# Layer 1's input projection with tokens on partitions: its two products turned in 32x32 blocks through DRAM, and the last projection begun two column blocks wide

## The chip, the cores and the metric

The kernel runs on one core of one Trainium2 chip. A time is the device time of one launch in microseconds (us). The verdict compares medians of runs of the two kernels taken on the same chip. Three runs of the kernel before gave 1809.98, 1813.17 and 1820.33 us.

The engines are named as in the profile: PE is the matrix engine (PEld its weight loads), DVE the vector engine, ACT the scalar engine, POOL and SP the other two. SP and ACT each have a hardware DMA queue; 16 DMA engines serve both. A name like L416 is line 416 of the kernel whose profile is quoted.

## What is computed

One step of a two-layer diffusion backbone over 256 latent tokens of width 2048. Layer 0 (neighbourhood attention and a state-space scan side by side) is not touched. Layer 1 is a gated short convolution:

```python
def short_conv_mixer(h, w_in, conv_w, w_out):
    p = h @ w_in                                  # (256, 2048) by (2048, 8192)
    bg, cg, hv, g = jnp.split(p, 4, axis=-1)
    y = bg * dw_conv(cg * hv, conv_w)             # 3 taps along the tokens
    return (jax.nn.silu(g) * y) @ w_out           # (256, 2048) by (2048, 2048)
...
x = x + gate[:, None] * y
```

All inputs and the output are fp32.

## The kernel before

**Products.** Every fp32 operand is split into a high part, rounded to the matrix engine's reduced fp32 format, and a low part, the difference. A product is three matmuls: high by high, low by high and high by low. Weights stream from DRAM in chunks of 512 KB (two blocks of 128 input rows by 512 columns) into one of five `raw` buffers; ACT makes the high part (`wH`, L409) and DVE the low part (`wL`, L416); three pairs of `wH`/`wL` buffers alternate. A chunk's low part frees the `raw` buffer, and the next load, issued on SP, goes into it. A chunk's last matmul frees its `wH` and `wL`, for the cast three chunks later.

**Two ways to multiply.** `mm_act` holds a block of 128 tokens of the activations as the stationary operand and streams 512 weight columns: tokens come out on the partitions, and a chunk takes 2 x 2 x 3 = 12 matmuls of 512 columns. `mm_both` holds a 128 x 128 weight block and streams the activations, high and low side by side (512 columns), and then the low weights against the high activations (256 columns): channels come out on the partitions, and a chunk takes 2 x 4 x 2 = 16 matmuls, half of 512 columns and half of 256. Layer 1's input projection uses `mm_both`; its results need channels on the partitions, since the convolution runs along the tokens. The output projection uses `mm_act`.

**Layer 1 before.** For each of four blocks `i` of 512 channels and each of the four parts (cg, hv, bg, g) the loop at L1770 takes four banks and eight chunks. `both` (L1715) empties a bank: ACT copies one half, DVE adds the other. `hv_gen` forms u = hv cg and the convolution into `v`, `bg_gen` multiplies by bg, `gg_gen` by silu(g) and splits the result into `y2` (high by ACT, L1766; low by DVE, L1767). The output projection (L1796) takes four column blocks of 512 one after the other, eight chunks each; its inner index is the channel block, so it needs the last channels' `y2` from its seventh chunk on.

**What sets the order.** The program is written in one pass. `Plan` keeps an estimated clock for each engine and for the data; generators hand out their steps when the clocks say that these are due (`may`, `pump`), and `force` drives them when a chunk can't go on. On the chip each engine then keeps the order that was written. Two details matter below. `Plan.keys` follows DRAM tiles in units of 256 elements, so two writes that share such a unit are planned one after the other. And beside layer 1's weights a matrix-vector product runs in the background (`gemv_gen`, L788): its blocks, 512 KB of `in_ada_w` each, share the `raw` buffers, and DVE multiplies them into `acc` (L803 before, L806 after, two instructions a block).

Of the kernel before, what the change touches and what calls it, by code (L numbers as in the profile page):

```python
# [10 lines left out]
AF = mybir.ActivationFunctionType  # L11
ALU = mybir.AluOpType
# [3 lines left out]
KB = 16  # L16
# [21 lines left out]
class Plan:  # L38
# [32 lines left out]
    def cost(self, e, op, i, ins, outs):  # L71
        n = max(self.size(a) for a in ins + outs)
        if e == "PE":
            n, cols = self.size(outs[0]), outs[0].ap[0][1]
            if i.is_transpose:
                return n / 1.2 + 3, 190
            if ins[0].dtype == F32R:
                return 9 + 0.434 * n, 190
            return 2 * max(55, n / 1.2) * (0.27 if cols == 32 else 0.52 if cols == 64 else 1) + (80 if cols < 128 else 0), 190
        if e == "DVE":  # L80
            if op == "Memset":
                return n * 0.26 + 60, 90
            if op in ("Reciprocal", "TensorReduce"):
                return n * 1.04 + 70, 90
            if len([a for a in ins if self.size(a) >= n]) >= 2 or op == "ISA" or self.psum(ins):
                return n * 1.22 + 70, 90
            return n * 0.6 + 130, 90
        if e == "ACT":
            return n * 0.85 + 150 + (200 if len(outs) > 1 else 0), 100
        if e == "POOL":  # L90
            return (n * 186 if n < 70 else n * 2.4) + 150, 60
        return 60, 0
# [49 lines left out]
def kernel(ctx: ExitStack, tc, x, cx, ada_w, ada_b, w_in, w_out, sc_in, sc_out, rpb, small, const,  # L142
# [7 lines left out]
    V, S, G, T, DMA = nc.vector, nc.scalar, nc.gpsimd, nc.tensor, nc.sync  # L150
    DMA2 = nc.scalar
    plan = Plan()
    E = plan.add
# [14 lines left out]
    def drt(shape, name):  # L168
        return dr.tile(list(shape), F32, name="dram_" + name)
# [3 lines left out]
    free_t = [st([128, 512], f"tmp{k}") for k in range(NTMP)]  # L173
    free_h = [st([128, 256], f"half{k}") for k in range(NHALF)]
    free_b = [pj.tile([128, 512], F32, tag=f"bank{k}", name=f"bank{k}", bufs=1) for k in range(8)]
# [17 lines left out]
    tmp, half, raw_ = (lambda: take(free_t)), (lambda: take(free_h)), (lambda: take(free_r))  # L193
# [11 lines left out]
    urgent, side, back = [], [], []  # L205
    got = set()
# [4 lines left out]
    def spawn(q, gen, tmps=0, halves=0):  # L211
        q.append(Task(gen, tmps, halves))
# [118 lines left out]
    def banks(n):  # L331
        force(lambda: len(free_b) >= n)
        return [take(free_b) for _ in range(n)]
# [4 lines left out]
    def give(pool, *bs):  # L338
        pool.extend(bs)

    W_ = lambda eng, *aps, nb=0: (eng, aps, nb)
    when = lambda f: ("if", f, 0)
# [40 lines left out]
    room = [2]  # L383

    def weight(w, r0, nb, c0, n):
        loads.append(("w", nw[0], w, r0, nb, c0, n, room[0]))
        nw[0] += 1
# [89 lines left out]
    def q_proj(w, c0, nc_, rows=D):  # L477
        room[0] = 2 if w is w_in and c0 >= COL_K else 1
        nb = 1024 // nc_
        for r0 in range(0, rows, nb * 128):  # L480
            weight(w, r0, nb, c0, nc_)
# [64 lines left out]
    for i in range(4):  # L546
        for part in (1, 2, 0, 3):
            q_proj(sc_in, part * D + i * 512, 512)
    for n in range(4):
        q_proj(sc_out, n * 512, 512)  # L550

    def rstd(o, s, n, eps, w):

# [107 lines left out]
    def chunk(kb0, kind, ps, first, last, lhs=None):  # L661

        H, Lo = use()
        nb = H.shape[1]
        for j in range(nb):
            kb = kb0 + j
            aH, aL = (hH[kb], hL[kb]) if lhs is None else lhs(kb)
            f, l = first and j == 0, last and j == nb - 1
            if kind == "act":
                mm_act(ps, aH, aL, H[:, j], Lo[:, j], f, l)  # L670
            elif kind == "both":
                mm_both(ps, aH, H[:, j], Lo[:, j], f, l)
            else:
                mm_ws(ps, aH, aL, H[:, j], Lo[:, j], kind, f, l)
        used()
# [774 lines left out]
    for k in range(2):  # L1450
        W, _ = use()
# [95 lines left out]
    h1 = {}  # L1547
# [104 lines left out]
    for ns in ((0, 512), (1024,), (1536,)):  # L1652
        pss = [banks(2) for n in ns]
        for ip in range(16):
# [8 lines left out]
            if hold[0]:  # L1663
# [6 lines left out]
                for t in range(2):  # L1670
                    for q, (H, Lo) in enumerate(ws):
                        for b in range(2):
                            i = 2 * order[NTAIL + q] + b
# [29 lines left out]
    y2 = [None] * KB  # L1703
# [1 line left out]
    flat = lambda ap, b: ap[:, 2 * b:2 * b + 2, :].rearrange("p b c -> p (b c)")  # L1705
    cg, u, v = st([128, 4, 256], "gt", name="cg"), st([128, 4, 256], "sz", name="u"), st([128, 4, 256], "QT", name="v")

    seq = [0]

    def ordered(k, gen):  # L1710
        yield when(lambda: seq[0] == k)
        yield from gen
        seq[0] += 1

    def both(p, o=None):  # L1715

        yield W_("ACT", p)
        o = half() if o is None else o
        E(S.copy(o, p[:, 256:]))
        yield W_("DVE", o)  # L1720
        E(V.tensor_tensor(out=o, in0=p[:, :256], in1=o, op=ALU.add))
        give(free_b, p)
        return o

    def cg_gen(i, ps):
        for b in range(4):
            yield from both(ps[b], cg[:, b, :])

    def hv_gen(i, ps):
        for b in range(4):  # L1730
            ch = 4 * i + b
            yield from both(ps[b], u[:, b, :])
            yield W_("DVE", u[:, b, :])
            E(V.tensor_tensor(out=u[:, b, :], in0=u[:, b, :], in1=cg[:, b, :], op=ALU.mult))
            yield W_("ACT", u[:, b, :])
            E(S.mul(v[:, b, :], u[:, b, :], scw[:, 1, ch:ch + 1]))
        for b in range(4):
            ch = 4 * i + b
            yield W_("DVE", v[:, b, :])
            E(V.scalar_tensor_tensor(out=v[:, b, 1:256], in0=u[:, b, 0:255], scalar=scw[:, 0, ch:ch + 1], in1=v[:, b, 1:256],  # L1740
                                     op0=ALU.mult, op1=ALU.add))
            E(V.scalar_tensor_tensor(out=v[:, b, 0:255], in0=u[:, b, 1:256], scalar=scw[:, 2, ch:ch + 1], in1=v[:, b, 0:255],
                                     op0=ALU.mult, op1=ALU.add))

    def bg_gen(i, ps):
        for b in range(4):
            bg = yield from both(ps[b])
            yield W_("DVE", bg, v[:, b, :])
            E(V.tensor_tensor(out=v[:, b, :], in0=bg, in1=v[:, b, :], op=ALU.mult))
            give(free_h, bg)  # L1750

    def gg_gen(i, ps):
        for b in range(4):
            kb = 4 * i + b
            gg = yield from both(ps[b])
            yield W_("ACT", gg)
            th = half()
            E(S.activation(th, gg, AF.Tanh, scale=0.5))
            yield W_("DVE", v[:, b, :])
            E(V.tensor_tensor(out=v[:, b, :], in0=gg, in1=v[:, b, :], op=ALU.mult))  # L1760
            yield W_("DVE", th)
            E(V.scalar_tensor_tensor(out=v[:, b, :], in0=th, scalar=1.0, in1=v[:, b, :], op0=ALU.add, op1=ALU.mult))
            give(free_h, gg, th)
            yield W_("ACT", v[:, b, :])
            hl = st([128, 2, 256], f"hH{kb}", F32R, name=f"y2_{kb}")
            E(S.copy(hl[:, 0], v[:, b, :]))  # L1766
            E(V.tensor_tensor(out=hl[:, 1], in0=v[:, b, :], in1=hl[:, 0].bitcast(F32), op=ALU.subtract))  # L1767
            y2[kb] = hl

    for i in range(4):  # L1770
        for part, gen in ((1, cg_gen), (2, hv_gen), (0, bg_gen), (3, gg_gen)):
            ps = banks(4)
            for kb in range(0, KB, 2):
                force(lambda: hL[kb + 1] is not None)
                chunk(kb, "both", ps, kb == 0, kb == KB - 2, lambda i: (h1[i], None))
            spawn(urgent, ordered(4 * i + (1, 2, 0, 3).index(part), gen(i, ps)), 0, {0: 1, 3: 2}.get(part, 0))

    def fin_gen(n, ps):
        cols = slice(n * 512, (n + 1) * 512)
        yield when(lambda: n_back[0] >= 15)  # L1780
        gb, o = tmp(), tmp()
        yield W_("SP", mrow[3:4])
        E(DMA.dma_start(gb, mrow[3, cols].partition_broadcast(128)))
        for t in range(2):
            if t:
                o = tmp()
            yield W_("DVE", ps[t], gb)
            E(V.tensor_tensor(out=o, in0=ps[t], in1=gb, op=ALU.mult))
            give(free_b, ps[t])
            E(V.tensor_tensor(out=o, in0=o, in1=x1[t][:, cols], op=ALU.add))  # L1790
            yield W_("SP", o)
            E(DMA.dma_start(out[t * 128:(t + 1) * 128, cols], o))
            give(free_t, o)
        give(free_t, gb)

    for n in range(4):  # L1796
        if n == 1:
            force(lambda: n_back[0] >= 15, (urgent, back))
        ps = banks(2)
        for kb in range(0, KB, 2):  # L1800
            force(lambda: y2[kb + 1] is not None)
            chunk(kb, "act", ps, kb == 0, kb == KB - 2, lambda i: (y2[i][:, 0], y2[i][:, 1]))
        spawn(urgent, fin_gen(n, ps), 3)
    force(lambda: not urgent, (urgent,))


# [50 lines left out]
```

## Time and profile before

| | us |
|---|---|
| median of three runs | 1813.17 |
| the profiled execution | 1814.06 |
| its span in the profile | 1812.3 |
| layer 1's input projection, first to last matmul start | 1359.7 to 1719.5 |
| output projection, first to last matmul start | 1719.6 to 1806.5 |

A row of the timeline gives start and length in us, engine, line, operation, output<-input, count, and in brackets the idle time ahead of it with what ended it. In a row of groups the numbers behind the bar are total busy time and the mean of one in ns. A matmul's length in the profile is its whole passage; matmuls follow each other faster than that, so their rate is read from their starts. A row of the windows gives a stretch, each engine's busy time (with instructions), the granted clock of the matrix engine as a fraction of full speed, the DMA engines' busy share and GB/s.

### The profile page before, as it was taken

The numbers are of one execution on the slowest core, as the hardware profiler recorded it, in microseconds if no ns is written. First come the engines' busy times: TensorE is split into PE (matmuls) and PEld (weight loads), VectorE is DVE, ScalarE is ACT, GpSimd is POOL, SyncE is SP. The second block draws the span as 40 slices with busy tenths as digits, with TensorE's granted clock in tenths as the row PEclk, the third lists the DMA queues.
The fourth block names the chain that finished last, engine by engine and source line by source line (L and its number), as shares of the span: only waits on it lengthen the run. The fifth ranks groups of instructions, "written<-read, shape, count | busy, mean of one in ns | idle before, by whom it ended". The sixth has DMA issues, their size and how long they took to land.

```text
span 1812.3 us, 26337 instructions
## 1 busy us (share of the span) xinstructions
PE 1775.1 (98%) x9961; PEld 1487.4 (82%) x9961; DVE 1259.2 (69%) x2041; ACT 775.3 (43%) x1362; POOL 30.5 (2%) x28
## 2 busy tenths in 40 slices
PE   5999999999999999999999999999999999999998
PEld 4677888888888888888888898778878888888887
DVE  5566875887575887575887687666667866665665
ACT  5422543455232455232454344544435444444442
POOL 0000100000000000000001000000000000000000
PEclk9999999999999999999999999999999999999999
DMA  9987654576655576655576566668776776666564
GB/s 337 342 289 254 196 163 135 169 217 202 204 168 168 170 220 198 218 165 169 170 221 186 165 185 185 205 211 300 268 248 203 241 231 188 190 192 188 192 211 153
DMA packets 249216, 376.90 MB, mean 208 GB/s; under 512 B 32656, under 2 KB 104048, under 8 KB 249088
## 3 DMA queue, kind: packets, MB, share of 16 engines
q1 hardware_dynamic: 239792, 366.64, 63.8%
q10 hardware_dynamic: 9296, 8.57, 1.4%
q8 instruction: 78, 1.28, 0.3%
q14 instruction: 50, 0.41, 0.1%
HBM read 368.70 MB, written 7.77 MB: 208 GB/s over the span
## 4 chain that ended last, share of the span: by engine, by line
PE 92%; DMA 3%; DVE 2%; issue 1%; ACT 1%; SPq 0%; POOL 0%; POOLq 0%; DVEq 0%; ACTq 0%
PE bank L198 90%; PE bank L202 3%; DMA raw<-in_ada_w 2%; DVE wL L416 1%; DVE acc L803 1%; DMA tmp<-dram_mixd 0%; DMA tmp<-dram_csr 0%; DVE hL L752 0%; SPq L566 0%; ACT wH L409 0%; DVE tmp L748 0%; ACT hH L746 0%; DVE xm L612 0%; ACT mix L1496 0%; DVE tmp L1790 0%
## 5 line engine op out<-in xcount | busy, mean ns | idle before, releaser
L409 ACT CAST wH<-raw 128x1024 fp32r<-128x1024 f32 (+1 forms) x440 | 459.0, 1044 | 701.2 <-PE bank L198 576.1
L416 DVE TENSOR_TENSOR wL<-raw,wH 128x1024 fp32r<-128x1024 f32 (+1 forms) x440 | 532.1, 1213 | 257.3 <-ACT wH L409 255.9
L198 PE MATMUL bank<-h,wH 128*128 128x512 f32 x1024 | 357.2, 395 | 2.7 <-ACT h L1636 1.5
L198 PE MATMUL bank<-hH,wH 128*128 128x256 f32 (+1 forms) x1040 | 352.6, 339 | 0.9 <-ACT wH L409 0.9
L198 PE MATMUL bank<-hL,wH 128*128 128x256 f32 (+1 forms) x1040 | 336.9, 324 | 0.0
L198 PE MATMUL bank<-hH,wL 128*128 128x256 f32 (+1 forms) x1024 | 331.2, 323 | 0.5 <-DVE wL L416 0.5
L198 PE MATMUL bank<-h,wL 128*128 128x256 f32 x1024 | 284.5, 278 | 0.0
L198 PE MATMUL bank<-wH,hH 128*128 128x512 f32 x640 | 257.4, 403 | 4.8 <-ACT hH L746 2.6
L198 PE MATMUL bank<-wL,hH 128*128 128x512 f32 x640 | 249.8, 391 | 0.3 <-DVE wL L416 0.3
L198 PE MATMUL bank<-wH,hL 128*128 128x512 f32 x640 | 249.3, 390 | 0.1
L803 DVE SCALAR_TENSOR_TENSOR acc<-raw,csil,acc 128x512 f32<-128x512 f32 x256 | 191.9, 750 | 65.5 <-DMA raw<-in_ada_w 52.0
L198 PEld LDWEIGHTS bank<-h,wH 128*128 128x128 f32 x1024 | 192.1, 188 | 49.1 <-issue 2.2
L198 PEld LDWEIGHTS bank<-hH,wH 128*128 128x128 f32 x1040 | 197.8, 190 | 23.2 <-issue 7.5
L198 PEld LDWEIGHTS bank<-hL,wH 128*128 128x128 f32 x1040 | 197.9, 190 | 19.8 <-issue 5.3
L198 PEld LDWEIGHTS bank<-hH,wL 128*128 128x128 f32 x1024 | 194.6, 190 | 16.5 <-DVE wL L416 1.1
L198 PEld LDWEIGHTS bank<-h,wL 128*128 128x128 f32 x1024 | 192.4, 188 | 0.0
L198 PE MATMUL bank<-wH,mix 128*128 128x512 f32 x512 | 164.1, 397 | 2.2 <-ACT wH L409 2.2
L198 PEld LDWEIGHTS bank<-wH,hH 128*128 128x128 f32 x640 | 120.2, 188 | 35.6 <-issue 7.5
L198 PEld LDWEIGHTS bank<-wH,hL 128*128 128x128 f32 x640 | 120.1, 188 | 25.4 <-DVE hL L752 0.6
L198 PEld LDWEIGHTS bank<-wL,hH 128*128 128x128 f32 x640 | 120.2, 188 | 24.3 <-DVE wL L416 1.1
L198 PEld LDWEIGHTS bank<-wH,mix 128*128 128x128 f32 x512 | 96.9, 189 | 23.4 <-ACT wH L409 2.7
L198 PE MATMUL bank<-wL,mix 128*128 128x512 f32 x256 | 100.6, 393 | 3.8 <-DVE wL L416 3.8
(244 smaller groups left out, 1662.9 us busy)
## 6 DMA issues: line engine op xcount, KB each, us to landing
raw<-in_w_in SPq DMA_DIRECT2D x209, 512.0 KB, 4.5
raw<-in_ada_w SPq DMA_DIRECT2D x163, 512.0 KB, 4.7
raw<-in_sc_in SPq DMA_DIRECT2D x128, 512.0 KB, 3.7
raw<-in_w_out SPq DMA_DIRECT2D x64, 512.0 KB, 4.3
raw<-in_sc_out SPq DMA_DIRECT2D x32, 512.0 KB, 4.5
tmp<-dram_csr SPq DMA_DIRECT2D x32, 256.0 KB, 7.1
PT<-in_ada_w SPq DMA_DIRECT2D x14, 512.0 KB, 5.8
yi<-in_ada_w SPq DMA_DIRECT2D x8, 512.0 KB
```

What stands on the lines that cost most here:

```text
L198: E(T.matmul(o, l, r, start=start, stop=stop, skip_group_check=True))
L202: E(T.transpose(o, i, ident if k == 128 else ident[:k, :k]))
L409: E(S.copy(H, v))
L416: E(V.tensor_tensor(out=Lo, in0=v, in1=H.bitcast(F32), op=ALU.subtract))
L803: E(V.scalar_tensor_tensor(out=acc, in0=v[:, j], scalar=csil[:, 2 * k + j:2 * k + j + 1], in1=acc, op0=ALU.mult, op1=ALU.add))
```

## The change

Layer 1's input projection uses `mm_act`: two banks of 128 tokens by 512 channels for each part. What then has to come back to channels on partitions is two products: cg hv, and bg silu(g). Each is formed with tokens on partitions, and DVE turns each 32 x 32 block in place (`V.transpose`, a STREAM_TRANSPOSE of 128 x 512). Four DMAs on ACT's queue for each token half write the blocks to a DRAM tile `trd` in runs of 32 elements (128 bytes), and one DMA fetches 512 channels by 256 tokens back (1 KB runs) into `u` or `cg`. Convolution and split then follow as before. The output projection runs column blocks 0 and 1 together, eight chunk pairs deep, and then 2 and 3 one at a time. The order of its weight loads follows, and the planner gets a price for the transpose.

```diff
-            if op in ("Reciprocal", "TensorReduce"):
+            if op in ("Reciprocal", "TensorReduce", "StreamTranspose"):
...
-    for n in range(4):
-        q_proj(sc_out, n * 512, 512)
+    for ns in ((0, 1), (2,), (3,)):
+        for kb in range(0, KB, 2):
+            for n in ns:
+                room[0] = 1
+                weight(sc_out, kb * 128, 2, n * 512, 512)
...
+    trd = drt([8, 512, 256], "trd")
+    def blocks(src, k, t):
+        yield W_("DVE", src)
+        tb = tmp()
+        E(V.transpose(tb, src))
+        give(free_t, src)
+        yield W_("AQ", tb)
+        for q in range(4):
+            E(DMA2.dma_start(bass.AP(tensor=trd.tensor, offset=trd[k].offset + t * 128 + q * 32,
+                                     ap=[[256, 32], [8192, 16], [1, 32]]),
+                             tb[32 * q:32 * q + 32].rearrange("p (b j) -> p b j", j=32)))
+        give(free_t, tb)
+    def fetch(dst, k):
+        yield W_("AQ", trd[k])
+        E(DMA2.dma_start(dst, trd[k].rearrange("(b p) q -> p b q", p=128)))
+    def row_gen(i, pC, pH):
...
+            E(S.copy(ct, pC[t]))
...
+            E(V.tensor_tensor(out=us[t], in0=pH[t], in1=us[t], op=ALU.mult))
...
+        for t in range(2):
+            yield from blocks(us[t], 2 * i, t)
+        yield ("cap", 0, 0)
+        yield when(lambda: i == 0 or ("gate", i - 1) in got)
+        yield from fetch(u, 2 * i)
...
+    def gate_gen(i, pB, pG):
...
+            yield W_("ACT", pG[t])
+            th = tmp()
+            E(S.activation(th, pG[t], AF.Tanh, scale=0.5))
+            yield W_("DVE", gs[t])
+            E(V.tensor_tensor(out=gs[t], in0=pG[t], in1=gs[t], op=ALU.mult))
+            give(free_b, pG[t])
+            yield W_("DVE", th)
+            E(V.scalar_tensor_tensor(out=gs[t], in0=th, scalar=1.0, in1=gs[t], op0=ALU.add, op1=ALU.mult))
+            give(free_t, th)
+            yield from blocks(gs[t], 2 * i + 1, t)
+        yield ("cap", 0, 0)
+        yield from fetch(cg, 2 * i + 1)
+        yield when(lambda: ("conv", i) in got)
...
     for i in range(4):
-        for part, gen in ((1, cg_gen), (2, hv_gen), (0, bg_gen), (3, gg_gen)):
-            ps = banks(4)
+        pss = []
+        for part in (1, 2, 0, 3):
+            ps = banks(2)
+            pss.append(ps)
             for kb in range(0, KB, 2):
                 force(lambda: hL[kb + 1] is not None)
-                chunk(kb, "both", ps, kb == 0, kb == KB - 2, lambda i: (h1[i], None))
-            spawn(urgent, ordered(4 * i + (1, 2, 0, 3).index(part), gen(i, ps)), 0, {0: 1, 3: 2}.get(part, 0))
+                chunk(kb, "act", ps, kb == 0, kb == KB - 2, lambda i: (h1[i][:, :256], h1[i][:, 256:]))
+            if part == 2:
+                spawn(urgent, row_gen(i, *pss), 3)
+                pss = []
+        spawn(urgent, gate_gen(i, *pss), 4)
...
+    for ns in ((0, 1), (2,), (3,)):
+        if ns[0]:
             force(lambda: n_back[0] >= 15, (urgent, back))
-        ps = banks(2)
+        pss = [banks(2) for _ in ns]
         for kb in range(0, KB, 2):
             force(lambda: y2[kb + 1] is not None)
-            chunk(kb, "act", ps, kb == 0, kb == KB - 2, lambda i: (y2[i][:, 0], y2[i][:, 1]))
-        spawn(urgent, fin_gen(n, ps), 3)
+            for ps in pss:
+                chunk(kb, "act", ps, kb == 0, kb == KB - 2, lambda i: (y2[i][:, 0], y2[i][:, 1]))
+        for n, ps in zip(ns, pss):
+            spawn(urgent, fin_gen(n, ps), 3)
```

How this moves instructions is not seen in the diff, since the planner decides it; three places follow. Lines behind 539 are shifted in the changed kernel (L803 is L806 there).

PE, at the first chunk of layer 1's input projection (`h_0` is channel block 0 of the activations, high and low in one tile; `wH` and `wL` the weights), before:

```order
L198 MATMUL bank_130<-h_0_10456,wH_136 128x512
L198 MATMUL bank_130<-h_0_10456,wL_139 128x256
L198 MATMUL bank_129<-h_0_10456,wH_136 128x512
L198 MATMUL bank_129<-h_0_10456,wL_139 128x256
L198 MATMUL bank_123<-h_0_10456,wH_136 128x512
L198 MATMUL bank_123<-h_0_10456,wL_139 128x256
```

and in the changed kernel:

```order
L198 MATMUL bank_130<-wH_136,h_0_10456 128x512
L198 MATMUL bank_130<-wL_139,h_0_10456 128x512
L198 MATMUL bank_130<-wH_136,h_0_10456 128x512
L198 MATMUL bank_129<-wH_136,h_0_10456 128x512
L198 MATMUL bank_129<-wL_139,h_0_10456 128x512
L198 MATMUL bank_129<-wH_136,h_0_10456 128x512
```

For a channel block and a part, four pairs of 512 and 256 columns have become six matmuls of 512.

DVE, beside the first blocks of layer 1, where the background product reads its `raw` buffers. Before, each reading stands behind other work since its buffer was last freed:

```order
L803 SCALAR_TENSOR_TENSOR acc<-raw_134,csil,acc 128x512 x2
L416 TENSOR_TENSOR wL_140<-raw_132,wH_137 128x1024
L1721 TENSOR_TENSOR u<-bank_124,u 128x256
L1734 TENSOR_TENSOR u<-u,cg 128x256
L416 TENSOR_TENSOR wL_141<-raw_133,wH_138 128x1024
L1721 TENSOR_TENSOR u<-bank_128,u 128x256
L1734 TENSOR_TENSOR u<-u,cg 128x256
L803 SCALAR_TENSOR_TENSOR acc<-raw_134,csil,acc 128x512
L416 TENSOR_TENSOR wL_139<-raw_131,wH_136 128x1024
```

In the changed kernel, at three spots in this order of the program:

```order
L416 TENSOR_TENSOR wL_140<-raw_135,wH_137 128x1024
L416 TENSOR_TENSOR wL_141<-raw_132,wH_138 128x1024
L806 SCALAR_TENSOR_TENSOR acc<-raw_132,csil,acc 128x512 x2
L416 TENSOR_TENSOR wL_139<-raw_133,wH_136 128x1024
...
L806 SCALAR_TENSOR_TENSOR acc<-raw_131,csil,acc 128x512 x2
L416 TENSOR_TENSOR wL_139<-raw_132,wH_136 128x1024
L806 SCALAR_TENSOR_TENSOR acc<-raw_131,csil,acc 128x512 x2
L416 TENSOR_TENSOR wL_140<-raw_133,wH_137 128x1024
...
L416 TENSOR_TENSOR wL_141<-raw_131,wH_138 128x1024
L806 SCALAR_TENSOR_TENSOR acc<-raw_135,csil,acc 128x512 x4
L416 TENSOR_TENSOR wL_139<-raw_133,wH_136 128x1024
```

The first L806 pair now stands directly behind the L416 that frees the buffer it reads; the second has one L416 between the reading that frees `raw_131` and the next reading of it; at the third, two blocks go through `raw_135` with nothing between them.

ACT, at the end of layer 1: the work that follows the last block of the last part until the last four `y2` are cast. Before, these casts stand among the first casts of the output projection's weights:

```order
L1758 ACTIVATE half_115<-half_118 128x256
L409 CAST wH_138<-raw_131 128x1024
L1766 CAST y_12_13298<-v 128x256
L1719 COPY half_122<-bank_124 128x256
L1758 ACTIVATE half_121<-half_122 128x256
L409 CAST wH_136<-raw_134 128x1024
L1766 CAST y_13_13332<-v 128x256
```

In the changed kernel, with `trd` the DRAM tile:

```order
L1721 DMA dram_trd<-tmp_113 32x16x32 x4
L409 CAST wH_136<-raw_134 128x1024
L409 CAST wH_137<-raw_132 128x1024
L409 CAST wH_138<-raw_131 128x1024
L1728 DMA cg<-dram_trd 128x4x256
L409 CAST wH_136<-raw_135 128x1024
L409 CAST wH_137<-raw_133 128x1024
L1788 CAST y_12_12910<-v 128x256
L1788 CAST y_13_12914<-v 128x256
L1788 CAST y_14_12927<-v 128x256
L409 CAST wH_138<-raw_134 128x1024
```

Three casts of weights stand between the last writes and the fetch, and two more between the fetch and the first of the last four `y2`. Counted from the end of layer 1's input projection, twelve casts stand ahead of `y_12`: those of the output projection's chunks 3 to 14 (from 0). Every other pair of writes and fetch in layer 1 has the same three casts between them.

More of the change, by code (lines that the diff above doesn't have):

```diff
@@ L1706 @@
     cg, u, v = st([128, 4, 256], "gt", name="cg"), st([128, 4, 256], "sz", name="u"), st([128, 4, 256], "QT", name="v")
[L1708 to L1729, printed above, removed]
+    trd = drt([8, 512, 256], "trd")
[14 more added lines that the diff above has]
+    def row_gen(i, pC, pH):
+        us = []
+        for t in range(2):
+            yield W_("ACT", pC[t])
+            ct = tmp()
+            E(S.copy(ct, pC[t]))
+            give(free_b, pC[t])
+            us.append(ct)
+        for t in range(2):
+            yield W_("DVE", pH[t], us[t])
+            E(V.tensor_tensor(out=us[t], in0=pH[t], in1=us[t], op=ALU.mult))
+            give(free_b, pH[t])
+        for t in range(2):
+            yield from blocks(us[t], 2 * i, t)
+        yield ("cap", 0, 0)
+        yield when(lambda: i == 0 or ("gate", i - 1) in got)
+        yield from fetch(u, 2 * i)
         for b in range(4):
             ch = 4 * i + b
-            yield from both(ps[b], u[:, b, :])
-            yield W_("DVE", u[:, b, :])
-            E(V.tensor_tensor(out=u[:, b, :], in0=u[:, b, :], in1=cg[:, b, :], op=ALU.mult))
             yield W_("ACT", u[:, b, :])
@@ L1743, in hv_gen @@
                                      op0=ALU.mult, op1=ALU.add))
[L1745 to L1752, printed above, removed]
+        got.add(("conv", i))
+    def gate_gen(i, pB, pG):
+        gs = []
+        for t in range(2):
+            yield W_("ACT", pB[t])
+            bt_ = tmp()
+            E(S.copy(bt_, pB[t]))
+            give(free_b, pB[t])
+            gs.append(bt_)
+        for t in range(2):
+            yield W_("ACT", pG[t])
[11 more added lines that the diff above has]
+        yield when(lambda: ("conv", i) in got)
         for b in range(4):
             kb = 4 * i + b
[L1755 to L1763, printed above, removed]
+            yield W_("DVE", v[:, b, :], cg[:, b, :])
+            E(V.tensor_tensor(out=v[:, b, :], in0=cg[:, b, :], in1=v[:, b, :], op=ALU.mult))
             yield W_("ACT", v[:, b, :])
@@ L1766, in gg_gen @@
             E(S.copy(hl[:, 0], v[:, b, :]))
+            yield W_("DVE", hl[:, 0])
             E(V.tensor_tensor(out=hl[:, 1], in0=v[:, b, :], in1=hl[:, 0].bitcast(F32), op=ALU.subtract))
             y2[kb] = hl
+        got.add(("gate", i))
     for i in range(4):
-        for part, gen in ((1, cg_gen), (2, hv_gen), (0, bg_gen), (3, gg_gen)):
-            ps = banks(4)
+        pss = []
+        for part in (1, 2, 0, 3):
+            ps = banks(2)
+            pss.append(ps)
             for kb in range(0, KB, 2):
                 force(lambda: hL[kb + 1] is not None)
-                chunk(kb, "both", ps, kb == 0, kb == KB - 2, lambda i: (h1[i], None))
-            spawn(urgent, ordered(4 * i + (1, 2, 0, 3).index(part), gen(i, ps)), 0, {0: 1, 3: 2}.get(part, 0))
+                chunk(kb, "act", ps, kb == 0, kb == KB - 2, lambda i: (h1[i][:, :256], h1[i][:, 256:]))
[3 more added lines that the diff above has]
+        spawn(urgent, gate_gen(i, *pss), 4)
     def fin_gen(n, ps):
@@ L1794, in fin_gen @@
         give(free_t, gb)
-    for n in range(4):
-        if n == 1:
+    for ns in ((0, 1), (2,), (3,)):
+        if ns[0]:
             force(lambda: n_back[0] >= 15, (urgent, back))
-        ps = banks(2)
+        pss = [banks(2) for _ in ns]
         for kb in range(0, KB, 2):
             force(lambda: y2[kb + 1] is not None)
-            chunk(kb, "act", ps, kb == 0, kb == KB - 2, lambda i: (y2[i][:, 0], y2[i][:, 1]))
-        spawn(urgent, fin_gen(n, ps), 3)
+            for ps in pss:
+                chunk(kb, "act", ps, kb == 0, kb == KB - 2, lambda i: (y2[i][:, 0], y2[i][:, 1]))
+        for n, ps in zip(ns, pss):
+            spawn(urgent, fin_gen(n, ps), 3)
     force(lambda: not urgent, (urgent,))
```

## The prediction

> **What bounds the kernel now.** I read the page's chain first, then that chain in order of time, and then the rate of the matmuls in the timeline.
>
> ```profile
> PE 92%; DMA 3%; DVE 2%; issue 1%; ACT 1%; SPq 0%; POOL 0%; POOLq 0%; DVEq 0%; ACTq 0%
> ...
> 1364.81 441.38 PE bank L198 x2429
> 1806.18 0.02 issue
> ```
>
> From 1364.81 to 1806.18 us, nearly all of layer 1, the chain is one unbroken row of matmuls: nothing else sets the end there. So the change can gain only in how fast matmuls follow each other, and can lose wherever it makes PE wait. The rate is read from starts in PE's timeline:
>
> ```profile
> 1714.42 0.40 PE L198 MATMUL bank<-h,wH 128*128 128x512 f32 x1
> ...
> 1719.27 0.40 PE L198 MATMUL bank<-h,wH 128*128 128x512 f32 x1
> ...
> 1802.15 0.39 PE L198 MATMUL bank<-wL,y 128*128 128x512 f32 x1
> ...
> 1806.23 0.39 PE L198 MATMUL bank<-wL,y 128*128 128x512 f32 x1
> ```
>
> The first two rows stand 14 pairs apart (512 and 256 columns): 4.85 / 14 = 0.346 us a pair. The other two stand six triples of `mm_act` apart, 18 matmuls of 512: 4.08 / 18 = 0.2267 us each. A chunk takes 8 pairs, 2.77 us, before, and 12 matmuls, 2.72 us, after.
>
> The clock is full in this stage, and the DMA engines are some 60% busy:
>
> ```profile
> 0.00:40.00 40.00, 22.12 (x145) 15.18 (x146) 21.05 (x61) 21.34 (x47) 1.86 (x7) 1.00 0.96 343
> 1630.00:1719.60 89.60, 89.60 (x518) 78.31 (x518) 56.19 (x77) 42.25 (x60) 0.00 (x0) 1.00 0.60 191
> ```
>
> How much delay PE can bear is in the rhythm of the weights, ACT's cast and DVE's low part of one chunk:
>
> ```profile
> 1714.15 1.05 ACT L409 CAST wH<-raw 128x1024 fp32r<-128x1024 f32 x1 [1.72 <-PE bank L198]
> ...
> 1715.24 1.23 DVE L416 TENSOR_TENSOR wL<-raw,wH 128x1024 fp32r<-128x1024 f32 x1 [1.55 <-ACT wH L409]
> ```
>
> ACT waits 1.72 us for PE to free a weight buffer and casts at once; the low part ends 2.3 us after the cast began. With three buffers, that chunk is needed two chunks later, 5.4 us. So a cast or low part may come **3.1 us** late before PE stops; ACT has 1.7 us of idle time a chunk on top.
>
> **The change part by part.** (1) *Matmuls.* 1024 pairs at 0.346 us (354.7 us) become 1536 matmuls at 0.2267 us (348.2 us): **-6.5 us**. The columns are the same, 786,432; what goes is the price per instruction of 512 fewer matmuls. It lies on the chain in full. The 5 us by which 359.8 us (1359.7 to 1719.5) exceed 354.7 are the wait for `h1` in the first chunks; the new form needs the same `h1` at 1.36 us a channel block for 1.38, so I leave them.
>
> (2) *Emptying the banks.* The rows of the groups in layer 1, and one from layer 0 for a copy of 512:
>
> ```profile
> L1721 DVE TENSOR_TENSOR half<-bank,half 128x256 f32<-128x256 f32 x32 | 13.4, 418 | 0.0
> L1719 ACT COPY half<-bank 128x256 f32<-128x256 f32 x32 | 10.6, 372 | 0.0
> L1760 DVE TENSOR_TENSOR v<-half,v 128x256 f32<-128x256 f32 x16 | 6.8, 422 | 0.2
> L1766 ACT CAST y<-v 128x256 fp32r<-128x256 f32 x16 | 6.4, 402 | 6.0 <-DVE v L1762 6.0
> L1767 DVE TENSOR_TENSOR y<-v,y 128x256 fp32r<-128x256 f32 x16 | 6.7, 422 | 3.6 <-ACT y L1766 3.6
> L1788 DVE TENSOR_TENSOR tmp<-bank,tmp 128x512 f32<-128x512 f32 x8 | 5.5, 686 | 6.4 <-PE bank L198 5.2 <-DMA tmp<-dram_mrow 1.2
> L1050 ACT COPY PT<-bank 128x512 f32<-128x512 f32 x8 | 4.5, 589 | 6.5 <-PE bank L202 6.5
> ```
>
> DVE loses 64 adds of 0.42 us and 64 products of 0.42 us, 54 us, and gains 24 operations of 512 at 0.69, 16 of 256 at 0.42 and the 16 transposes. No row shows a transpose; the row above for 512 elements, 0.69, is nearest, 0.42 (half the elements) and 1.23 (the low part's 1024) are the ends. That makes 34 us, 31 to 43 at the ends. ACT loses 64 copies and 16 activations of 256 (some 30 us) and gains 24 of 512 (14 us). Both are idle for over a third of the stage in the window's row, so this is **nothing**; if DVE had no gaps, the 20 us saved would be a gain, and if the transposes fell wrong, each could delay a low part by 1.2 us, inside the 3.1.
>
> (3) *Writes and fetches.* 64 writes and 8 fetches, all on ACT's queue, none in layer 1 on it before but four small ones.
>
> ```profile
> L998 SPq DMA_DIRECT2D bias<-dram_rpbs x64: 573/615/641, 230.2 to 1170.1; - x64
> L921 ACTq DMA_DIRECT2D dram_mixd<-half x32: 321/354/752, 280.8 to 1200.6; - x32
> ```
>
> A write has three dimensions as the first row's (615 ns to issue; the second's two dimensions, 354, are the lower end). Four take 2.5 us behind a cast. The next cast is due 2.72 us after the last one: beside ACT's own 1.05 and 1.72 us the issue is hidden. At 1.2 us each it would be 2 us late, inside the 3.1. What a 128-byte packet costs, no row shows. Nearest are the 256-byte rows of the `bias` loads, here with 5 us of the trace around eight of them:
>
> ```profile
> DMA packets 1896, 0.85 MB, mean 171 GB/s; under 512 B 1384, under 2 KB 1896, under 8 KB 1896
> ...
> q1 hardware_dynamic: 1896, 0.85, 67.0%
> ```
>
> 67% of 16 engines for 5 us is 53.6 us. The 512 larger packets carry 0.50 MB; at the first window's rate (343 / 16 / 0.96 = 22.3 bytes a ns and engine) they take 22 us, which leaves 31 us for 1384 small ones, **23 ns** each. By bytes alone a packet of 128 would take 6. I take 23: four writes are 2048 packets, 128 an engine, 2.9 us. Sixteen such groups and eight fetches (1.5 us each at that rate) add 59 us to 360, a share of 0.6 becoming 0.76. A fetch stands three casts, 8.2 us, behind its last writes. With 40% of the engines free the writes take 7.4 us and the rest of a landing 2.0 (below: 2.7 less 0.35 to issue and 0.4 of data): 9.4 us, 1.2 late, inside ACT's 1.7 of idle time. So **nothing**; the lower end is nothing too, the upper one is a rival.
>
> (4) *The background product.* The planner has put three L806 readings behind the very L416 or L806 that frees their buffer. The trace has one such load nearly alone:
>
> ```profile
> 1393.71 0.37 SPq L379 DMA_DIRECT2D raw<-in_ada_w  x1
> ...
> 1396.55 1.23 DVE L416 TENSOR_TENSOR wL<-raw,wH 128x1024 fp32r<-128x1024 f32 x1 [1.55 <-ACT wH L409]
> 1399.10 1.54 DVE L803 SCALAR_TENSOR_TENSOR acc<-raw,csil,acc 128x512 f32<-128x512 f32 x2 [1.32 <-DMA raw<-in_ada_w]
> 1400.56 1.22 DVE L416 TENSOR_TENSOR wL<-raw,wH 128x1024 fp32r<-128x1024 f32 x1
> ...
> raw<-in_ada_w SPq DMA_DIRECT2D x163, 512.0 KB, 4.7
> raw<-in_sc_in SPq DMA_DIRECT2D x128, 512.0 KB, 3.7
> tmp<-dram_csr SPq DMA_DIRECT2D x32, 256.0 KB, 7.1
> dram_mixd<-half ACTq DMA_DIRECT2D x32, 128.0 KB, 2.7
> ```
>
> From issue to use took 5.4 us, and DVE, which keeps its order, stood 1.3 us with the next L416 queued behind it. In the changed order, counted from the end of the last L416: at the first spot the next one ends after 5.4 + 1.5 (the reading) + 1.2 = 8.1 us where 2.7 is the rhythm, 5.4 late, less 3.1: PE stops 2.3 us. At the second, with one L416 between, 1.5 + 5.4 + 1.5 + 1.2 = 9.7 against 5.4: 1.1 us. At the third, two blocks through one buffer, 9.7 against 2.7: 3.9 us. Together **+7.3 us**. With the 3.7 us of the `in_sc_in` loads it is 2.8, with the longest landing above, 7.1, it is 12.4; I take 5.4, the same load in the same stage.
>
> (5) *The end of layer 1.* Block `y_12` is needed when chunk 11 of the output projection ends. Its cast stands behind that of chunk 14, which waits for chunk 11 to free a buffer. So the high part is there 1.05 + 0.40 = 1.5 us after chunk 11 ends, and the low part, behind the L416 of chunk 14, after 2.3 + 0.4 = 2.7. PE can do two matmuls (0.45) in between: it loses **+2.3 us**. Block 13 follows in 1.3 us (0.42, 0.40, 0.42), as fast as PE needs it. If the fetch took 7.1 us, its data would come 2.7 us after chunk 11 ends, and PE would lose up to 5.
>
> (6) *Two blocks wide.* Column blocks 0 and 1 together give the last `y2` twelve chunks, 32.6 us, instead of six. Without it the whole of the turn would stand before PE; with it only (5) is left. The final column block and what follows 1806 us are as before.
>
> Sum: -6.5 + 7.3 + 2.3 = +3.1. From the profiled 1814.06 us that is 1817.2. The median of the runs is 0.9 lower; the three spread over 10 us, so I round: **1817 us**.
>
> **Rivals.** *The waits are hidden* (0.16): the landing is nearer 3.7 us and the three spots and the end cost almost nothing. The page's chain speaks for it, in which L803 stood before too and PE never stopped; against it, those readings had other work ahead of them. 1814.1 - 6.5 = 1808; with the 5 us at the stage's start also gone, 1803.
>
> *The small writes block ACT's queue* (0.23), the slower side: at twice the price, 46 ns, a group of writes takes 5.9 us of the engines, 14.7 us beside the loads, 16.7 with the rest of the landing. The fetch, behind it on ACT's queue, is 8.5 us late, with three casts behind it; less 1.7 and 3.1 PE stops 3.7 us at each of eight, 30 us: 1847. It decides from some 30 ns on, where 128 packets at 40% exceed 8.2 + 1.7 us less the 2.0. For it: no row shows many writes below 1 KB. Against it: 23 ns covers twice the bytes. The Trainium skill's page "DMA: Bandwidth & Descriptors", section Specifications, says that below 512 bytes a DMA engine reads, modifies and writes; by that rule the doubling is what to expect. No run here shows it: the 256-byte rows are reads of DRAM.
>
> *The rate does not come* (0.08): `mm_act` in this stage, with new loads of h1, keeps 0.231 us a matmul (two thirds of a pair's 0.346). Then (1) is nothing and 1823.7. The rate of the output projection speaks against it.
>
> The forecast itself has 0.47, and 0.06 is left for what I don't see.
>
> **How the numbers follow.** A measurement here tells about 0.5%, 9 us, from no change: 1804 and 1822. Faster is the best part of the first rival, 0.05. Slower are the small writes (0.23), the missing rate (0.08), the upper part of the forecast, which reaches 1814.1 - 6.5 + 12.4 + 5 = 1825 (0.11), and half of what I don't see: 0.45. The same is 0.50. The range runs from 1807, just below the first rival, to 1842, within the second; the forecast's own is 1810 to 1825.
>
> **What would show it.** PE's starts in layer 1 at 0.227 us; DVE waits "L806 <- DMA raw" of 3 to 6 us at three places in the first 140 us of the stage and PE waits on L416 behind them; a PE wait for `y_12` some 33 us into the output projection. The fetches' landing, and ACT waits for `dram_trd` ahead of casts, decide about the second rival. I am wrong if PE waits regularly in all four channel blocks, or if no wait stands at those places.

## The result, and the profile after

| us | before | after |
|---|---|---|
| median of 20 runs each | 1814.79 | 1820.04 |
| lowest and highest | 1809.27 to 1823.11 | 1816.88 to 1827.38 |
| span of the profiled execution | 1812.3 | 1817.3 |
| layer 1, from its first matmul's start to its last | 1359.69 to 1806.46: 446.8 | 1359.51 to 1811.56: 452.1 |
| of it the input projection | 359.9 | 362.7 |
| of it the output projection | 86.8 | 89.4 |

The ratio of after to before is 1.0032 (95% interval 1.0019 to 1.0044): 5 to 6 us slower, which is inside the 0.5% that the prediction called no change, and clear of noise all the same. The whole difference lies in layer 1: up to its first matmul the two profiles agree within 0.2 us, and from there to the last matmul the new one takes 5.3 us more. Of all the runs in this document one, of the kernel one_wide below, took 8775.86 us and is left out of its numbers.

The chain of waits after the change: its shares by engine, and then rows of it in order of time (start, length in us, what set the end in that stretch). Before, one row of matmuls ran unbroken from 1364.81 to 1806.18 us.

```profile
PE 86%; DMA 6%; DVE 5%; ACT 2%; issue 1%; SPq 0%; POOL 0%; DVEq 0%; POOLq 0%; ACTq 0%
...
1381.79 38.77 PE bank L198 x175
1420.59 1.06 ACT wH L409
1421.67 1.24 DVE wL L416
1422.92 5.21 DMA raw<-in_ada_w
1428.23 0.76 DVE acc L806
1429.68 1.23 DVE wL L416
1430.95 23.46 PE bank L198 x95
...
1456.99 0.70 DVE tmp L1773
...
1480.56 4.38 DMA raw<-in_ada_w
1485.04 0.76 DVE acc L806
1486.49 1.23 DVE wL L416
1487.76 267.23 PE bank L198 x1183
1755.01 1.05 ACT wH L409
1756.09 1.22 DVE wL L416
1757.70 53.58 PE bank L198 x235
```

The chain leaves PE where a load of the background product stands in it, with its L806 behind it and an L416 that PE needs behind that, and once more at 1755, before `y_12`. Between them matmuls set the end again, 267 us in one piece through the last three channel blocks. The writes and fetches are nowhere on it. Of the new work with tokens on partitions a little is: ahead of the second stop, from 1455.39 to 1458.41 us, ACT's L1765 and L1771 and DVE's L1773 and L1776 stand in the chain.

PE's waits from 1340 us on, by what ended them (us in total, times, longest):

```profile
PE bank L198 <- DVE wL L416: 9.5, 5, 3.1
...
PE bank L198 <- ACT y L1788: 1.4, 1, 1.4
...
PE bank L198 <- DVE y L1790: 0.6, 1, 0.6
```

Of the 9.5 us, 1.6 lie ahead of layer 1. Before, the first row was 1.2 us, all of it ahead of layer 1, and there were no rows of `y`. DVE's timeline at the second place, and SP's row of the load that it waits for:

```profile
1455.52 1.23 DVE L416 TENSOR_TENSOR wL<-raw,wH 128x1024 fp32r<-128x1024 f32 x1 [1.50 <-ACT wH L409]
1456.99 0.69 DVE L1773 TENSOR_TENSOR tmp<-bank,tmp 128x512 f32<-128x512 f32 x1 [0.24 <-ACT tmp L1771]
1457.71 0.69 DVE L1776 SCALAR_TENSOR_TENSOR tmp<-tmp,tmp 128x512 f32<-128x512 f32 x1
1458.44 0.71 DVE L1717 STREAM_TRANSPOSE tmp<-tmp 128x512 f32<-128x512 f32 x1
1459.08 1.18 DVE L416 TENSOR_TENSOR wL<-raw,wH 128x1024 fp32r<-128x1024 f32 x1
1460.18 1.53 DVE L806 SCALAR_TENSOR_TENSOR acc<-raw,csil,acc 128x512 f32<-128x512 f32 x2
1461.63 1.22 DVE L416 TENSOR_TENSOR wL<-raw,wH 128x1024 fp32r<-128x1024 f32 x1
1468.00 1.54 DVE L806 SCALAR_TENSOR_TENSOR acc<-raw,csil,acc 128x512 f32<-128x512 f32 x2 [5.16 <-DMA raw<-in_ada_w]
1469.46 3.49 DVE L416 TENSOR_TENSOR wL<-raw,wH 128x1024 fp32r<-128x1024 f32 x3
...
1461.74 0.37 SPq L379 DMA_DIRECT2D raw<-in_ada_w  x1
```

The row at 1468.00 is the mechanism: DVE stands 5.2 us for a load that was issued only when DVE itself had freed the buffer, and three L416 then follow without a gap, the sign that they had been due.

### The profile page after: what moved, and what is told of

Same layout as the page of the kernel before. It is cut to its first block, busy times and chain, and to the rows that moved or that the text cites. A ratio compares the mean times of both kernels' runs of the same rounds, so it can differ in the third digit from the quotient of the medians.

```text
span 1817.3 us, 25261 instructions
## 1 busy us (share of the span) xinstructions
PE 1771.7 (97%) x9449; PEld 1465.5 (81%) x9449; DVE 1242.5 (68%) x1969; ACT 764.1 (42%) x1306; POOL 31.5 (2%) x28
## 4 chain that ended last, share of the span: by engine, by line
PE 86%; DMA 6%; DVE 5%; ACT 2%; issue 1%; SPq 0%; POOL 0%; DVEq 0%; POOLq 0%; ACTq 0%
PE bank L198 83%; DMA raw<-in_ada_w 3%; PE bank L202 3%; DVE wL L416 2%; DMA tmp<-dram_csr 1%; DVE acc L806 1%; DMA tmp<-dram_mixd 1%; ACT wH L409 1%; DMA raw<-in_w_out 1%; DVE hL L755 0%; DVE tmp L1348 0%; SPq L569 0%; DVE h L1620 0%; DVE tmp L751 0%; DVE tmp L1359 0%
## 5 line engine op out<-in xcount | busy, mean ns | idle before, releaser
L416 DVE TENSOR_TENSOR wL<-raw,wH 128x1024 fp32r<-128x1024 f32 (+1 forms) x440 | 530.8, 1212 | 264.1 <-ACT wH L409 261.6
L198 PE MATMUL bank<-wH,h 128*128 128x512 f32 x1024 | 318.2, 392 | 2.1 <-DVE h L1620 1.7
L806 DVE SCALAR_TENSOR_TENSOR acc<-raw,csil,acc 128x512 f32<-128x512 f32 x256 | 192.0, 750 | 82.9 <-DMA raw<-in_ada_w 67.5
L198 PEld LDWEIGHTS bank<-wH,h 128*128 128x128 f32 x1024 | 192.8, 189 | 43.5 <-DVE h L1620 2.9
L198 PE MATMUL bank<-wL,h 128*128 128x512 f32 x512 | 200.5, 392 | 7.8 <-DVE wL L416 7.8
L198 PEld LDWEIGHTS bank<-wL,h 128*128 128x128 f32 x512 | 96.6, 189 | 29.6 <-DVE wL L416 9.5
```

Source lines behind the costliest of these rows:

```text
L198: E(T.matmul(o, l, r, start=start, stop=stop, skip_group_check=True))
L416: E(V.tensor_tensor(out=Lo, in0=v, in1=H.bitcast(F32), op=ALU.subtract))
L806: E(V.scalar_tensor_tensor(out=acc, in0=v[:, j], scalar=csil[:, 2 * k + j:2 * k + j + 1], in1=acc, op0=ALU.mult, op1=ALU.add))
```

## The experiments

All of them are edits of the changed kernel, but for the control, which is an edit of the kernel before. Ratios are to the kernel before, on the same chip.

### The background product handed out later, and its control

```diff
         if hor < 2000:
             rdy += 4000 if eng == "PE" else 0
+            if eng == "DVE" and gapb[0]:
+                return t <= now + hor and rdy + gapb[0] <= now
...
     trd = drt([8, 512, 256], "trd")
+    gapb[0] = 3000
```

`now` is PE's planned clock and `rdy` the planned landing; `gapb` is 0 until layer 1 begins. The control, before_late, is the kernel before with the same lines.

> The changed kernel with one rule more: from layer 1 on the planner hands out a reading of the background product only when its load has been due for 3 us by PE's clock, so other L416 stand between the reading that frees a raw buffer and the next reading of it. Theory (order on DVE): the profile of the changed kernel shows PE stopped behind L806 three times, at 1428, 1468 and 1484 us, 2.0 + 2.5 + 3.1 us of idle time and some 2.5 us in restarts and slow matmuls behind the first; these 10 us go, the wait for y_12 (2.4 us) stays: 1810 us, ratio to the kernel before 0.995 to 0.998. Rival (the small writes make the loads late, so that the waits only move): PE's waits for L416 stay over 6 us and the time stays at 1817 or more.

> The kernel before with the rule of bg_later alone, as its control. Theory: there PE waits only 1.2 us for L416 in this stage, so the time stays within 1.5 us of the kernel before, 0.999 to 1.001. Rival (the rule is a gain of its own, and bg_later says nothing on the change): it falls by 5 us or more, to 0.997 or less.

bg_later: 1811.57 us, 0.9976 (0.9962 to 0.9991). before_late: 1816.23 us, 0.9998 (0.9987 to 1.0010). In bg_later DVE waits for no `in_ada_w` load in layer 1, and its chain is matmuls from the first chunks to the last `y2`:

```profile
1386.37 363.06 PE bank L198 x1611
...
1752.14 55.15 PE bank L198 x235
```

From 1.0032 to 0.9976 is 0.56%, 10 us, as the stops were priced, and the rule gives the old kernel nothing. So the loss was the order that the planner happened to write around the change, not the change, and without it the change gains. The profiled execution of bg_later was the slowest of its twelve runs; its layer 1 still takes 8.6 us less than that of the changed kernel.

### The last fetch three casts earlier

```diff
+        if n.startswith("dram_trd") and ap.offset >= 7 * 512 * 256:
+            k, c = divmod(ap.offset, 512 * 256)
+            return [(n, 8 * k + j) for j in (range(8) if a[-1][1] == 256 else [c // 32])]
...
         yield ("cap", 0, 0)
+        at = pos["split"]
+        yield when(lambda: i < 3 or pos["split"] >= at + 3)
         yield from fetch(cg, 2 * i + 1)
```

The first piece is in `Plan.keys`: the planner no longer takes the four writes of the last product for one after the other. The second keeps three casts between these writes and their fetch.

> The kernel of bg_later, and the planner follows the four writes of the last product one by one, so that it places the last two groups of writes, their fetch and the y_12 to y_15 casts three weight casts earlier. Theory: the PE wait for y_12 (1.6 + 0.7 us and restarts, 2.5 us) goes too: 1807 to 1808 us, 0.994 to 0.996 of the kernel before, the 6 us that the matmuls save being left nearly whole. Rival (the fetch itself is too slow, whatever its place): y_12 is still waited for and the time equals bg_later within 0.7 us.

1808.99 us, 0.9965 (0.9951 to 0.9978), 2.6 us less than bg_later. The two intervals overlap, so the runs alone don't separate these two kernels; the profiles do, since bg_later waits 2.0 us for `y_12` and bg_fetch doesn't wait there. ACT's row of the `y_12` cast, which stood at 1755.96 in the changed kernel, and the row of the chain that covers layer 1:

```profile
1738.87 0.41 ACT L1797 CAST y<-v 128x256 fp32r<-128x256 f32 x1
```
```profile
1383.00 416.74 PE bank L201 x1848
```

From 1383.00 to 1799.74 PE never stops. From layer 1's first matmul to its last are 439.3 us, 7.5 less than before. By its interval this version is faster than the kernel before, by 0.35%, and it is faster than the changed kernel.

### One column block at a time

```diff
-    for ns in ((0, 1), (2,), (3,)):
+    for ns in ((0,), (1,), (2,), (3,)):
```

The line stands twice, for the loads and for the products.

> The changed kernel with the output projection in four column blocks one after the other, and its weight loads in that order; all else as in the changed kernel. Theory: y_12 is then needed 16.3 us after the output projection's first matmul in place of 32.6; in the changed kernel it is there after 34.2 us, so PE stops some 14 us longer than the 2.5 us now, less if the planner starts the last fetch earlier: 1828 to 1836 us. Rival (the fetch and the casts are paced by PE's chunks and come as early as they are needed): within 2 us of the changed kernel, 1820.

1833.35 us, the median of three runs, 1.0086 (1.0061 to 1.0111). PE's wait for the first late `y2`:

```profile
PE bank L198 <- ACT y L1788: 13.3, 1, 13.3
```

13.3 us in place of 2.0. In the profiles the output projection takes 103.3 us in place of 89.4: beginning two blocks wide hides 14 us in this kernel. The ratios, from three runs, differ by 0.54%, some 10 us, with an uncertainty of 5.

### The size of the writes

Five kernels with every engine's order as in the changed kernel, in which the four writes of a token half are laid down in runs of another length. The bytes are the same, but they lie in another order in DRAM, so the fetch brings the blocks back in the wrong places and the output is another: these kernels leave out the right order of the blocks and tell of times alone. For 64 bytes:

```diff
-                                     ap=[[256, 32], [8192, 16], [1, 32]]),
-                             tb[32 * q:32 * q + 32].rearrange("p (b j) -> p b j", j=32)))
+                                     ap=[[4096, 32], [128, 32], [1, 16]]),
+                             tb[32 * q:32 * q + 32].rearrange("p (b j) -> p b j", j=16)))
```

> The changed kernel, every engine's order unchanged, with the four writes of a token half laid down in runs of 512 elements (2 KB) in place of 32 (128 bytes): the same bytes, 2048 packets in place of 32768, in another order in DRAM, so that the fetches bring the blocks back unturned and the output is another. Theory (order on DVE): PE's stops behind the background product stand where they stood, 7 to 8 us in all, since the readings still sit behind the freeing L416: 1817 to 1821 us. Rival (the small packets make the in_ada_w loads late): the stops shrink to under 3 us and the time falls to 1813 or less.

> The same with runs of 16 elements (64 bytes): 65536 packets, output again another. In the changed kernel ACT's queue took 9.8% of 16 engines in the 401 us from 1359 on, 629 us; less 188 us for the 4.2 MB of fetches at 22.3 bytes a ns that leaves 441 us, 13.4 ns a 128-byte packet. Price by packet: 878 us for the writes, four of them 3.4 us of all engines, some 9 us beside the loads, at the edge of the three casts: 1821 to 1827 us. Price by byte: as the changed kernel, 1820.

> The same with runs of 8 elements (32 bytes): 131072 packets, so that 128 bytes cost 54 ns if the price is by packet, past the 30 ns from which the prediction's second rival decides. By packet: four writes 6.9 us of all engines, 17 us beside the loads, the fetch late by 9 us or more, PE stopped some 4 to 6 us at each of eight fetches, 1850 to 1870 us. By byte: 1820. If the packets do double but the fetch hides them all the same, under 1830, the second rival's bound was wrong.

> As runs2k with runs of 128 elements (512 bytes), 8192 packets, output again another. From runs2k, the changed kernel, runs64 and runs32 (6.0, 9.8, 13.8 and 18.5% of 16 engines for ACT's queue in the 401 us from 1359 on) a write costs about 7.5 ns and its bytes at 22.3 a ns. By that line: 8192 x 30.5 = 250 us and 193 for the fetches, 6.9%. [...] Time as the changed kernel by both, 1816 to 1822 us.

> The same with runs of 64 elements (256 bytes), 16384 packets. By the line of runs512: 16384 x 19 = 311 us and 193, 7.9%. [...] Time as the changed kernel by both.

ACT's queue from 1359 to 1760 us (packets, MB, share of 16 engines), runs of 2048, 512, 256, 128 (the changed kernel), 64 and 32 bytes in this order, one row of each kernel:

```profile
q10 hardware_dynamic: 7312, 8.40, 6.0%
```
```profile
q10 hardware_dynamic: 13456, 8.40, 6.8%
```
```profile
q10 hardware_dynamic: 21617, 8.37, 7.7%
```
```profile
q10 hardware_dynamic: 38032, 8.40, 9.8%
```
```profile
q10 hardware_dynamic: 68548, 7.76, 13.8%
```
```profile
q10 hardware_dynamic: 123141, 7.47, 18.5%
```

| run of | 2048 | 512 | 256 | 128 | 64 | 32 bytes |
|---|---|---|---|---|---|---|
| writes | 2048 | 8192 | 16384 | 32768 | 65536 | 131072 |
| time, us | 1818.07 | 1815.87 | 1825.55 | 1820.04 | 1829.86 | 1850.75 |
| ratio to before | 1.0013 | one run | one run | 1.0032 | 1.0068 | 1.0190 |

The intervals are 1.0000 to 1.0026 for 2048 bytes, 1.0040 to 1.0096 for 64 and 1.0159 to 1.0222 for 32; 512 and 256 are one run each, beside a run of the kernel before of 1813.59.

Three things follow. *The order, not the small packets, makes the first stops*: with a sixteenth of the writes' packets PE still waits 6.0 us for L416 in layer 1, for 7.8 in the changed kernel, and 2.5 for `y_12`. The difference of some 2 us is the part that the packets can have in it; between single profiles it isn't shown to be theirs.

*The price of a packet* is close to a line, without a step: 7.5 ns for each packet of the writes, and the bytes of writes and fetches at 22.3 a ns, gives 6.1, 6.8, 7.8 and 9.7% for the first four; 64 and 32 bytes, where one fetch or a few writes fall outside the window, come to 13.1 and 19.0. A write of 128 bytes costs (9.8% of 6416 us, less 188 for the fetches) / 32768 = 13.4 ns, one of 64 bytes about 11. The Trainium skill's page "DMA: Bandwidth & Descriptors", section Specifications, has engines read, modify and write below 512 bytes. The section gives no price for it. If it doubled the price by bytes, which is 23 ns for a write of 512, then one of 256 bytes would cost 23 ns too, and the shares would be 5.9% at 512 bytes and 8.9% at 256, an estimate from the 22.3 bytes a ns; 6.8 and 7.7 show no such step.

*What small writes block first is ACT*. Its timeline with runs of 32 bytes:

```profile
1565.08 1.05 ACT L411 CAST wH<-raw 128x1024 fp32r<-128x1024 f32 x1 [1.67 <-PE bank L200]
1565.09 7.33 ACTq L1723 DMA_DIRECT2D dram_trd<-tmp  x4
1572.52 2.95 ACT L411 CAST wH<-raw 128x1024 fp32r<-128x1024 f32 x3 [6.38 <-issue]
...
1588.61 2.94 ACT L411 CAST wH<-raw 128x1024 fp32r<-128x1024 f32 x3 [7.13 <-PE bank L200]
1592.20 0.38 ACTq L1730 DMA_DIRECT2D cg<-dram_trd  x1
```

and the same place in the changed kernel:

```profile
1567.33 1.05 ACT L409 CAST wH<-raw 128x1024 fp32r<-128x1024 f32 x1 [1.66 <-PE bank L198]
1567.34 2.14 ACTq L1721 DMA_DIRECT2D dram_trd<-tmp  x4
```

Issuing four writes takes 2.1 us with 512 packets each and 7.3 here, with 2048 each; the next casts queue behind it, three of them then run without a gap, and PE stops in every channel block. The fetch is late too: by the trace's semaphore record the last of its writes landed at 1592.13, the fetch is issued right behind at 1592.20, 1.7 us after the third cast began (1590.51), and in the changed kernel the same fetch is issued 0.2 us after that cast began. That costs nothing by itself, since ACT's next cast, at 1595.32, waits for PE. With runs of 64 bytes the four take some 4.6 us, and from 1505 to 1760 us PE waits nowhere: its extra time is all at the first stops, at `y_12` and in slow matmuls behind them (below). Its median, 1829.86, lies 3 us above the range that was expected.

## Why the prediction was right, step by step

It said 1817 us, +3.1, no change by its bound; measured are 1820.04 and +5.3. The range and the likeliest case held, and the places were the ones named.

**Matmuls, -6.5.** Right. Two starts of PE after the change, 98 matmuls apart, give 22.22 / 98 = 0.2267 us each:

```profile
1699.73 0.39 PE L198 MATMUL bank<-wH,h 128*128 128x512 f32 x1
...
1721.95 0.39 PE L198 MATMUL bank<-wH,h 128*128 128x512 f32 x1
```

bg_fetch, in which PE has no other stop, is 7.5 us shorter in layer 1 than the profile before and 0.35% faster in its runs, 6.4 us. The old form has two rates: by their starts, 32 pairs take 11.09 us in some stretches and 11.31 in others, in both profiles of it. The prediction took the faster one. The control's profile has more of the slower, and its projection took 362.5 us against 359.9. The rival of a missing rate is out.

**Emptying the banks, nothing.** The transpose takes 0.70 us, 0.69 was taken (the lower end of the sum is 30 us, not 31). "Nothing" holds for three channel blocks of four. At the second spot it doesn't: L1773, L1776 and L1717 above push the L416 at 1459.08 back by 0.8 us (2.72 after 1455.52 it was due), and this adds to a delay that already reaches PE.

**Writes and fetches, nothing.** Right in the sum, wrong in the price: 13.4 ns for the 23 taken from reads of 256 bytes. At 64 bytes, 22 ns for each 128, the kernel shows what the prediction said for 23: no wait in the later blocks. The four issues lie beside the cast, as the rows at 1567 show (both begin together), and not behind it. The engines' share in the stage, 0.76, came out as forecast, but by luck. It rose by 0.11 and not by 0.16, and the 0.60 that was taken for the share before is that of the last 90 us alone; the same 319 us before and after are:

```profile
1400.00:1719.00 319.00, 319.00 (x1844) 277.69 (x1843) 211.54 (x291) 149.52 (x210) 0.00 (x0) 1.00 0.65 204
```
```profile
1400.00:1719.00 319.00, 311.33 (x1375) 256.03 (x1374) 194.18 (x224) 138.75 (x161) 0.00 (x0) 0.99 0.76 224
```

**The background product, +7.3.** PE's three waits were 2.0, 2.5 and 3.1 us for 2.3, 1.1 and 3.9, 7.7 in all; they are gone in bg_later, whose one edit moves the readings. The second was sized too low by the 0.8 above and by a load that took 6.3 us to its use (1461.74 to 1468.00) for 5.4; the third too high by a load that took 4.5. What the term lacked is what comes behind a stop: a restart of 0.3 us each (by the starts, the second stop costs PE 2.8 us with an idle time of 2.5), and 1.6 us of matmuls at half the clock after the first. With these it is 10.2 us, 2.9 more than the sum had for it; the matmuls gave 1.0 of that back.

**The end of layer 1, +2.3.** PE waits 1.4 and 0.6 us, 2.6 with restarts. The mechanism was half the story:

```profile
1749.79 0.38 ACTq L1728 DMA_DIRECT2D cg<-dram_trd  x1
...
1755.01 1.04 ACT L409 CAST wH<-raw 128x1024 fp32r<-128x1024 f32 x1 [1.66 <-PE bank L198]
1755.96 0.40 ACT L1788 CAST y<-v 128x256 fp32r<-128x256 f32 x1
...
1755.50 0.43 DVE L1785 TENSOR_TENSOR v<-cg,v 128x256 f32<-128x256 f32 x1 [0.90 <-DMA cg<-dram_trd]
```

The cast does stand behind that of chunk 14, and the fetch, 5.7 us to its use, would have held it to the same moment: L1785 ends at 1755.93. bg_fetch moved both; which one alone would do was not tried.

**Two wide.** The profile of one_wide puts 14 us on it.

**The rival of the small writes** (1847) needed a price past 30 ns for 128 bytes, and the chip has 13.4. Its own terms give other bounds than 30: 7.9 us at 40% are 25 ns for a late fetch, and 34 with the 3.1 us that PE can bear. The runs agree: at 22 ns no later block stops, and at 35 ns (1187 us of the queue, less seven fetches, over some 118,000 packets, times four for 128 bytes) the kernel is 30 us slower than the changed one, the size that the rival gave. Its path was half right: the fetch is late, by 1.5 us in the rows above, but what stops PE are the casts behind ACT's issuing.

In sum: -7.5 + 10.2 + 2.6 = +5.3, as measured in layer 1; that the total came within 3 us also owes something to errors of opposite sign.

## What to carry to other kernels

A change that moves little work can still cost a background task its place: look for a reading that stands directly behind the instruction that frees its own buffer, on an engine that keeps its order, because there the whole latency of the load comes into the open. Price a stop of PE with what follows it, not only with its length. A planner that judges readiness by an optimistic landing (its formula gives 3.9 us for a load of 512 KB alone, and the four that DVE stood for took 4.5 to 6.3) needs a margin for work that isn't urgent; here 3 us of margin were worth 10.

## What was not expected of the hardware

After some stops PE's granted clock falls to a half, in these profiles for 3.4 or 6.8 us (13.7 with the stop of 13.3 us, most of it inside the stop). Windows behind stops (PE busy, then the other engines, granted clock, DMA share, GB/s), after the change behind its first, second and third stop of 2.0, 2.5 and 3.1 us:

```profile
1431.00:1435.00 4.00, 4.00 (x11) 3.12 (x12) 2.17 (x2) 0.00 (x0) 0.00 (x0) 0.57 1.06 394
...
1470.00:1475.00 5.00, 4.27 (x19) 3.55 (x20) 4.93 (x7) 1.06 (x1) 0.00 (x0) 1.00 0.82 267
1487.00:1492.00 5.00, 4.24 (x24) 3.12 (x25) 3.18 (x4) 0.83 (x1) 0.00 (x0) 1.00 0.88 293
```

and with runs of 512 bytes behind stops of 1.0 and 3.7 us:

```profile
1462.00:1467.00 5.00, 4.05 (x18) 3.36 (x19) 4.93 (x6) 2.39 (x3) 0.00 (x0) 1.00 0.80 260
1480.00:1486.00 6.00, 5.44 (x19) 3.64 (x20) 3.07 (x4) 0.00 (x0) 0.00 (x0) 0.50 0.88 281
```

Over the profiles of after, bg_later, one_wide and the runs of 2048, 512, 256 and 64 bytes, 13 of the 15 single stops of 1.9 us or more in the places treated here came with such a stretch, and one of the ten shorter ones; a stretch cost 1.6 to some 3 us. The profiled execution with 2 KB runs had 10.2 us at half clock in layer 1 and the changed kernel's 3.4: it waits 1.9 us less at the first stops, and its layer 1 still takes 1.1 us more. That execution was the slowest of its ten, so this needn't hold for the others. The Trainium skill's page "TensorE: Matmul & The Clock Gate", in Part 1, tells of a half clock after an idle window of about 3.4 us, in windows that run freely; the stops here were enough from 1.9 us on. What decides about the two that had no such stretch wasn't tried.
